# Second SwiGLU stage of a hybrid layer: the high weights meet both operand parts in one 512-column matmul

## The chip, the core and the metric

The kernel runs on one core of a Trainium2 chip. The metric is the device time of one execution in microseconds (us). TensorE (PE) multiplies; a matmul holds 128x128 weights that a separate weight load (PEld) has put there, and streams the columns of the other operand past them into a bank of PSUM. VectorE (DVE) and ScalarE (ACT) read PSUM and SBUF, each working through its own queue in order. GpSimd (POOL) has no part in the stage that is changed. SyncE (SP) issues the DMAs.

## The reference

One layer on x of 256 tokens by 1024 features, in float32: a SwiGLU stage, a mixer (a diagonal state-space branch and an attention branch), a second SwiGLU stage, a final norm.

```python
def swiglu(h, w_gate, w_up, w_down):
    return (jax.nn.silu(h @ w_gate) * (h @ w_up)) @ w_down
...
    h = rmsnorm(x, ffn1_norm[l])
    x = x + 0.5 * swiglu(h, ffn1_w_gate[l], ffn1_w_up[l], ffn1_w_down[l])
    h = rmsnorm(x, mix_norm[l])
    x = x + hybrid_mixer(h, w_in[l], ...)
    h = rmsnorm(x, ffn2_norm[l])
    x = x + 0.5 * swiglu(h, ffn2_w_gate[l], ffn2_w_up[l], ffn2_w_down[l])
return rmsnorm(x, final_norm)
```

The inner width D_FF is 2816, so each of the stage's three weight matrices is 8 x 22 = 176 tiles of 128x128.

## The kernel before

Activations lie with features on the partitions and the 256 tokens (T) along the columns. Every float32 operand of a large product is split into a high part that TensorE's fp32r format holds exactly and the low rest: weights into `wh` and `wl`, activations into `xh` and `xl` (stage input, tile `xhl`) or `ah` and `al` (gated product, tile `ahl`). A weight tile then takes three matmuls of 256 columns into the same PSUM bank, wh·xh, wh·xl and wl·xh, lines 188 to 190 of `mm3`; called a triple here. wl·xl is left out.

The weights come from HBM as one stream of units, 8 tiles (512 KB) each, in the order in which they are used. ScalarE makes `wh` of a unit (line 90, `wh<-stage`) and VectorE `wl` (line 78, `wl<-stage,wh`). `weight(n)` calls `ahead(u)` when TensorE's program reaches unit u; that issues wh of unit u+4, wl of unit u+3, the load of unit u+6 and the postponed subtractions `al = gs - ah`. Both rings hold five units. The order of the instructions on each engine is the order in which the code is written (`manual_schedule`).

The second SwiGLU stage is `ffn(f2, idle, FH2, 4, after_ffn2, 2)`, with g = 2, one part and kh = 22. A gate or an up product takes 8 weight tiles (K = 1024), which is one unit, and goes to a bank of its own: gate products to `ps_m` (`mm`, 3 banks), up products to `ps_a` (`mma`, 3 banks). The first four products (gate 0, up 0, gate 1, up 1) run interleaved over k. Then come gate 2 and up 2; two weight tiles into up 2, `catch_up` spreads the norm's factor over the partitions (`ips`, copied to `inv`) and the six products that are waiting are worked off: gate bank times inv, Silu, times up bank, copy to `ah`:

```python
            def finish(j, gs, up):
                tt(gs, gs, up)
                act(ah[:, j, :], gs)
                deferred.append(lambda o=al[:, j, :], a=gs, b=ah[:, j, :]: tt(o, a, b, ALU.subtract))

            def gated(gp):
                gs = ev.tile([128, T], F32, name="gs", tag="gs", bufs=3)
                tt(gs, gp, inv)
                act(gs, gs, AF.Silu)
                return gs
```

From gate 3 on each product is worked off when it ends. After the 22 pairs come eight down products of 22 tiles (2.75 units) each, whose results are scaled into `dn` (line 87) and added to x (tile `xg`). Products are numbered from 0 here.

Of the kernel before, what the change touches and what calls it, by code (L numbers as in the profile page):

```python
# [10 lines left out]
F32 = mybir.dt.float32  # L11
# [3 lines left out]
ALU = mybir.AluOpType  # L15
# [3 lines left out]
T = 256  # L19
D = 1024  # L20
KD = D // 128
# [12 lines left out]
X_AT = (48, 48, 48)  # L34
A_AT = (48, 0, 0)
# [26 lines left out]
def hybrid_layer(ctx: ExitStack, tc: tile.TileContext, xT, wst, consts, bc, out):  # L62
    nc = tc.nc
    V, S, G, PE = nc.vector, nc.scalar, nc.gpsimd, nc.tensor
# [7 lines left out]
    ps_m = ctx.enter_context(tc.tile_pool(name="ps_m", bufs=3, space=PSUM))  # L72
    ps_s = ctx.enter_context(tc.tile_pool(name="ps_s", bufs=2, space=PSUM))
    ps_a = ctx.enter_context(tc.tile_pool(name="ps_a", bufs=3, space=PSUM))
    ctx.enter_context(tc.manual_schedule())

    def tt(out, a, b, op=ALU.mult, eng=None):
        (eng or V).tensor_tensor(out=out, in0=a, in1=b, op=op)  # L78
# [7 lines left out]
    def stt(out, a, s, b, op0, op1):  # L86
        V.scalar_tensor_tensor(out=out, in0=a, scalar=s, in1=b, op0=op0, op1=op1)

    def act(out, a, func=AF.Copy, **kw):
        S.activation(out=out, in_=a, func=func, **kw)  # L90
# [17 lines left out]
    inv = cp.tile([128, T], F32, name="inv")  # L108
# [57 lines left out]
    def ahead(u):  # L166
        split_hi(u + LA)
        split_lo(u + LA - 1)
        load_to(u + LA + 2)
        while deferred:  # L170
            deferred.pop(0)()
        if u in hooks:
            hooks.pop(u)()

    def weight(n, cnt=1):
        u, s = divmod(n, UT)
        if u > state["at"]:
            state["at"] = u
            if u not in state["hold"]:
                ahead(u)  # L180
        h, lo = split[u]
        return h[:, s * 128:(s + cnt) * 128], lo[:, s * 128:(s + cnt) * 128]

    pos = [0]

    def mm3(ps, n, xh, xl, start, stop):
        wh, wl = weight(n)
        PE.matmul(ps, wh, xh, start=start, stop=False)  # L188
        PE.matmul(ps, wh, xl, start=False, stop=False)  # L189
        PE.matmul(ps, wl, xh, start=False, stop=stop)  # L190

    def gemm(xh, xl, nk, ps=None, side={}):
        if ps is None:
            ps = ps_m.tile([128, T], F32, name="mm", tag="mm")
        for k in range(nk):
            mm3(ps, pos[0] + k, xh[:, k, :], xl[:, k, :], k == 0, k == nk - 1)
            if k in side:
                side[k]()
        pos[0] += nk
        return ps  # L200


    xhl = cp.tile([128, 2 * KD * T + SLACK], F32R, name="xhl")

    def placed(t, n, o):
        return [t[:, o + i * n * T:o + (i + 1) * n * T].rearrange("p (k t) -> p k t", k=n) for i in range(2)]

    xv = [placed(xhl, KD, o) for o in X_AT]

    def split_x(k, g):  # L210
        xh, xl = xv[g]
# [21 lines left out]
    def norm(pool=ps_a, tag="at", diag=True, between=None):  # L233
        ps = [pool.tile([128, 1], F32, name="nps", tag=tag) for _ in range(2)]
        terms = [acc] + squares
        squares.clear()
        for n, a in enumerate(terms):
            if between and n == len(terms) - 1:
                between()
            for i in range(2):  # L240
                for o in (0, 64):
                    PE.matmul(ps[i][o:o + 64, :], a[:, i * 128 + o:i * 128 + o + 64], ones[:, 0:1],
                              start=n == 0, stop=n == len(terms) - 1)
        v, t, y = nrm[:, 0, :], nrm[:, 1, :], inv_tm
        for i in range(2):
            ts(v[:, i:i + 1], ps[i], 1.0 / D, ALU.mult, RMS_EPS, ALU.add)
        ts(y.bitcast(I32), v.bitcast(I32), -0.5, ALU.mult, RSQRT_MAGIC, ALU.add)
        gram(t, y, v)
        stt(y, t, RSQRT_B, y, ALU.subtract, ALU.mult)
        gram(t, y, v)  # L250
        ts(v, t, -0.375 * RSQRT_A ** 5, ALU.mult, 1.25 * RSQRT_A ** 3, ALU.add)
        tt(v, v, t)
        stt(y, v, 1.875 * RSQRT_A, y, ALU.subtract, ALU.mult)
        if diag:
            diags.append(ev.tile([128, 2, 128], F32, name="dg", tag="sq"))
            for i in range(2):
                ts(diags[0][:, i, :], ident, y[:, i:i + 1], ALU.mult)
# [3 lines left out]
    def spread(pool=ps_a, tag="at", copy=V.tensor_copy):  # L261
        ps = pool.tile([128, T], F32, name="ips", tag=tag)
        PE.matmul(ps, ones, diags.pop().rearrange("p a b -> p (a b)"), start=True, stop=True)
        copy(inv, ps)
        return ps


    def psum(i):
        if i % 2:
            return ps_a.tile([128, T], F32, name="mma", tag="at")  # L270
        return ps_m.tile([128, T], F32, name="mm", tag="mm")

    def ffn(pool, bg, parts, norm_at, done, g):
        kh = KF // parts
        xh, xl = xv[g]
        for f in range(parts):
            ahl = pool.tile([128, 2 * kh * T + SLACK], F32R, name="ahl", tag="ahl")
            ah, al = placed(ahl, kh, A_AT[g])
            def finish(j, gs, up):
                tt(gs, gs, up)  # L280
                act(ah[:, j, :], gs)
                deferred.append(lambda o=al[:, j, :], a=gs, b=ah[:, j, :]: tt(o, a, b, ALU.subtract))

            def gated(gp):
                gs = ev.tile([128, T], F32, name="gs", tag="gs", bufs=3)
                tt(gs, gp, inv)
                act(gs, gs, AF.Silu)
                return gs

            for j in range(kh):  # L290
                if f == 0 and j < 2:
                    if j == 0:
                        first = [psum(i) for i in range(4)]
                        for k in range(KD):
                            for i in range(4):
                                mm3(first[i], pos[0], xh[:, k, :], xl[:, k, :], k == 0, k == KD - 1)
                                pos[0] += 1
                            if k == norm_at:
                                norm(ps_s, "s5")
                                if state["at"] in state["hold"]:  # L300
                                    ahead(state["at"])
                    if j == 0:
                        continue
                    gate = gemm(xh, xl, KD, psum(0))
                else:
                    if f > 0 or j > 2:
                        gate = gemm(xh, xl, KD, psum(0))
                        gs, side = gated(gate), {}
                        if f > 0 or j < kh - 2:
                            bg()  # L310
                    else:
                        def catch_up():
                            spread(ps_s, "s5", act)
                            for i in range(2):
                                finish(i, gated(first[2 * i]), first[2 * i + 1])
                            if state["at"] in state["hold"]:
                                ahead(state["at"])

                        side = {1: catch_up}
                    up = gemm(xh, xl, KD, psum(1), side)  # L320
                    if side:
                        gs = gated(gate)
                    finish(j, gs, up)
                if f > 0 or j < kh - 2:
                    bg()
            for m in range(KD):
                ps = gemm(ah, al, kh)
                t = ev.tile([128, T], F32, name="dn", tag="sg")
                stt(t, ps, 0.5, inv, ALU.mult, ALU.mult)
                tt(x[:, m, :], t, x[:, m, :], ALU.add)  # L330
                if f == parts - 1:
                    done(m)
                bg()
# [566 lines left out]
    with tc.tile_pool(name="tab", bufs=1) as tab:  # L900
        with tc.tile_pool(name="f1", bufs=1) as f1:
            gen = s5_build(f1, tab)
            next(gen)

            def after_ffn1(m):
                split_x(m, 1)
                square(m, m == 0)


            calls = [0]  # L910

            def bg():
                calls[0] += 1
                if calls[0] > BG_FROM:
                    next(gen, None)

            ffn(f1, bg, FH1, 6, after_ffn1, 0)
            for _ in gen:
                pass
        with tc.tile_pool(name="mx", bufs=1) as mxp:  # L920
            mixer(mxp, tab)
    with tc.tile_pool(name="f2", bufs=1) as f2:
# [22 lines left out]
        for h in range(2):  # L945
            o = f2.tile([128, 2, 512], F32, name=f"out{h}")
# [115 lines left out]
```

## Time and profile before

| what | value |
|---|---|
| time, median of 3 runs | 558.54 us (558.08 to 563.71) |
| the profiled execution's own time | 557.2 us |
| its span, first to last instruction | 555.3 us |
| mean granted clock of TensorE | 0.995 |
| TensorE busy, weight loads busy | 544.5 us (98%), 534.5 us (96%) |
| VectorE busy, ScalarE busy | 399.2 us (72%), 309.1 us (56%) |
| first matmul of the second SwiGLU stage | 364.47 us |
| last start of a matmul of its down products | 545.09 us |

The span and everything in the trace are of the one profiled execution; 1.9 us of its time lie outside the span. Matmuls overlap in their pipeline, so the pace of a stream of them is read from the distance of two starts, not from the duration of one.

### The profile page before, as it was taken

The page shows a single profiled execution, that of the slowest core. Times are in us where ns is not written, and L with a number is a line of the kernel's source. Part 1 is how long each engine was busy: PE and PEld are TensorE (multiplying, and loading weights), DVE is VectorE, ACT ScalarE, POOL GpSimd, SP SyncE. Part 2 cuts the span into 40 slices and gives each one's busy share as a digit, 9 for nine tenths or more (in the row PEclk, how much of TensorE's full clock was granted, in tenths as well). Part 3 has the DMA queues.
Part 4 walks back from the last instruction along what each step waited for, and adds up shares of the span by engine and source line. Part 5 has one row for each costly group of instructions (what it writes and reads, how often), then busy time and mean ns, then how long its engine had stood idle before and what let it go on. Part 6 is the DMA issues. An engine that isn't in the chain of part 4 may idle for free.

```text
span 555.3 us, 11894 instructions
## 1 busy us (share of the span) xinstructions
PE 544.5 (98%) x4860; PEld 534.5 (96%) x4860; DVE 399.2 (72%) x657; ACT 309.1 (56%) x477; POOL 80.3 (14%) x150
## 2 busy tenths in 40 slices
PE   7999999999999999999999999999999999999994
PEld 7999999999999989989999999999999999999994
DVE  5886798888865776999845888786766666665643
ACT  7764546559575683336547665565555444455421
POOL 0288951957000000000000000000000000000000
PEclk9999999999999999999999999999999999999998
DMA  8876666557564445265342656564755555666502
GB/s 281 297 253 195 193 194 216 156 157 229 175 201 159 145 152 152 77 208 191 105 145 77 203 185 186 187 209 164 228 195 192 191 190 193 194 210 204 173 15 77
DMA packets 28678, 99.30 MB, mean 179 GB/s; under 512 B 3152, under 2 KB 3792, under 8 KB 28624
## 3 DMA queue, kind: packets, MB, share of 16 engines
q1 hardware_dynamic: 28624, 98.54, 55.0%
q8 instruction: 38, 0.62, 0.4%
q14 instruction: 16, 0.13, 0.1%
HBM read 97.48 MB, written 1.05 MB: 177 GB/s over the span
## 4 chain that ended last, share of the span: by engine, by line
PE 94%; DVE 3%; DMA 1%; issue 1%; SPq 0%; DVEq 0%; ACT 0%
PE mm L188 20%; PE mm L189 19%; PE mm L190 19%; PE mma L188 8%; PE mma L189 8%; PE mma L190 8%; PE bps L615 1%; PE sps L714 1%; DMA stage<-in_wst_dram 1%; PE yps L662 1%; PE ops L744 1%; DVE wl L78 1%; PE up L584 1%; PE up L586 1%; PE vp L586 1%; PE vp L585 1%
## 5 line engine op out<-in xcount | busy, mean ns | idle before, releaser
L78 DVE TENSOR_TENSOR wl<-stage,wh 128x1024 fp32r<-128x1024 f32 (+2 forms) x187 | 223.3, 1201 | 15.0 <-ACT wh L90 14.8
L90 ACT ACTIVATE wh<-stage 128x1024 fp32r<-128x1024 f32 (+2 forms) x187 | 191.5, 1030 | 56.3 <-PE mm L189 26.3
L188 PE MATMUL mm<-xhl,wh 128*128 128x256 f32 x544 | 152.1, 280 | 2.2 <-ACT wh L90 2.2
L190 PE MATMUL mm<-xhl,wl 128*128 128x256 f32 x544 | 150.9, 277 | 0.4 <-DVE wl L78 0.4
L189 PE MATMUL mm<-xhl,wh 128*128 128x256 f32 x544 | 150.4, 277 | 0.0
L188 PEld LDWEIGHTS mm<-xhl,wh 128*128 128x128 f32 x544 | 102.1, 188 | 3.5 <-ACT wh L90 2.4
L190 PEld LDWEIGHTS mm<-xhl,wl 128*128 128x128 f32 x544 | 102.2, 188 | 1.0 <-DVE wl L78 0.8
L189 PEld LDWEIGHTS mm<-xhl,wh 128*128 128x128 f32 x544 | 102.2, 188 | 0.1
L188 PE MATMUL mma<-xhl,wh 128*128 128x256 f32 x352 | 97.7, 278 | 0.0
L188 PE MATMUL mm<-ahl,wh 128*128 128x256 f32 x352 | 97.5, 277 | 0.0
L190 PE MATMUL mm<-ahl,wl 128*128 128x256 f32 x352 | 97.2, 276 | 0.0
L189 PE MATMUL mm<-ahl,wh 128*128 128x256 f32 x352 | 97.2, 276 | 0.0
L189 PE MATMUL mma<-xhl,wh 128*128 128x256 f32 x352 | 97.2, 276 | 0.0
L190 PE MATMUL mma<-xhl,wl 128*128 128x256 f32 x352 | 97.2, 276 | 0.0
L188 PEld LDWEIGHTS mm<-ahl,wh 128*128 128x128 f32 x352 | 66.1, 188 | 0.2 <-issue 0.2
L188 PEld LDWEIGHTS mma<-xhl,wh 128*128 128x128 f32 x352 | 66.1, 188 | 0.1
L189 PEld LDWEIGHTS mma<-xhl,wh 128*128 128x128 f32 x352 | 66.1, 188 | 0.1
L190 PEld LDWEIGHTS mm<-ahl,wl 128*128 128x128 f32 x352 | 66.1, 188 | 0.0
L189 PEld LDWEIGHTS mm<-ahl,wh 128*128 128x128 f32 x352 | 66.1, 188 | 0.0
L190 PEld LDWEIGHTS mma<-xhl,wl 128*128 128x128 f32 x352 | 66.0, 188 | 0.0
L90 ACT ACTIVATE gs<-gs 128x256 f32<-128x256 f32 x52 | 21.8, 418 | 54.1 <-DVE gs L78 53.8
L78 DVE TENSOR_TENSOR gs<-gs,mma 128x256 f32<-128x256 f32 x44 | 18.5, 419 | 38.5 <-PE mma L190 33.7
(214 smaller groups left out, 730.8 us busy)
## 6 DMA issues: line engine op xcount, KB each, us to landing
stage<-in_wst_dram SPq DMA_DIRECT2D x178, 512.0 KB, 3.7
stage<-in_wst_dram SPq DMA_DIRECT2D x7, 256.0 KB, 5.5
out_dram<-out SPq DMA_DIRECT2D x2, 512.0 KB, 3.2
xg<-in_xT_dram SPq DMA_DIRECT2D x3, 256.0 KB, 5.8
bct<-in_bc_dram SPq DMA_DIRECT2D x1, 512.0 KB, 5.5
cst<-in_consts_dram SPq DMA_DIRECT2D x1, 396.0 KB, 4.7
stage<-in_wst_dram SPq DMA_DIRECT2D x2, 128.0 KB, 2.5
xg<-in_xT_dram SPq DMA_DIRECT2D x1, 144.0 KB, 2.1
```

Source lines behind the costliest of these rows:

```text
L78: (eng or V).tensor_tensor(out=out, in0=a, in1=b, op=op)
L90: S.activation(out=out, in_=a, func=func, **kw)
L188: PE.matmul(ps, wh, xh, start=start, stop=False)
L189: PE.matmul(ps, wh, xl, start=False, stop=False)
L190: PE.matmul(ps, wl, xh, start=False, stop=stop)
L584: PE.matmul(acc2[i], xh[:, k, sl], wh, start=k == 0, stop=False)
L585: PE.matmul(acc2[i], xh[:, k, sl], wl, start=False, stop=False)
L586: PE.matmul(acc2[i], xl[:, k, sl], wh, start=False, stop=k == KD - 1)
L615: PE.matmul(bp[part][o, gp, :], Rt[part][:, 8 * h + gp, o], Uc[:, 8 * h + gp, :], start=True, stop=True)
L662: PE.matmul(ypf[64 * par:64 * par + 64, gg, :], l, r.rearrange("p a b -> p (a b)"), start=term == 0, stop=term == 2)
L714: PE.matmul(sps[e][:, blk, :].rearrange("p a b -> p (a b)"), q[r, i, qs], k[r, i, ks], start=part == 0, stop=part == 1)
L744: PE.matmul(op[:, i, e, :], pq[:, b, :], v[:, j, h, :], start=j == 0, stop=b != 1)
```

## The change

Only the second SwiGLU stage (g = 2) is changed. The high and the low part of its operands are laid side by side for each k (`paired`), so that one 512-column matmul `wh · [xh | xl]` writes wh·xh into the first half of a bank and wh·xl into the second; `wl · xh` stays a 256-column matmul into the first half (`mmw`, `gemmw`). A triple thus becomes a pair, with two weight loads in place of three. For the first k of a product the wide matmul comes first, for the others the narrow one. Each result now is the sum of a bank's halves, made by `fold`: ScalarE copies the second half to SBUF, VectorE adds the first. That is done for the 44 gate and up products and for seven of the eight down products; the last down product keeps the triples. 352 + 7 x 22 = 506 triples are replaced, and 51 folds added.

```diff
@@ mm3, after it
+    def mmw(ps, n, y, start, stop):
+        wh, wl = weight(n)
+
+        def high():
+            PE.matmul(ps, wh, y, start=start, stop=stop)
+
+        if start:
+            high()
+        PE.matmul(ps[:, 0:T], wl, y[:, 0:T], start=False, stop=False)
+        if not start:
+            high()
+
+    def gemmw(y, nk, ps, side={}):
+        for k in range(nk):
+            mmw(ps, pos[0] + k, y[:, k, :], k == 0, k == nk - 1)
+            if k in side:
+                side[k]()
+        pos[0] += nk
+        return ps
@@ placed, after it
+    def paired(t, n, o):
+        return t[:, o:o + 2 * n * T].rearrange("p (k t) -> p k t", k=n)
+
+    def halves(y):
+        return y[:, :, 0:T], y[:, :, T:]
+
+    xw = paired(xhl, KD, X_AT[2])
+    xv = [placed(xhl, KD, o) for o in X_AT[:2]] + [halves(xw)]
@@ ffn
+            def fold(ps):
+                if g < 2:
+                    return ps
+                c = pool.tile([128, T], F32, name="fold", tag="fold", bufs=4)
+                act(c, ps[:, T:])
+                tt(c, ps[:, 0:T], c, ALU.add)
+                return c
+
+            def product(i, side={}):
+                if g < 2:
+                    return gemm(xh, xl, KD, psum(i), side)
+                return gemmw(xw, KD, psum(i, 2 * T), side)
...
-                tt(gs, gs, up)
+                tt(gs, gs, fold(up))
...
-                tt(gs, gp, inv)
+                tt(gs, fold(gp), inv)
...
-                ps = gemm(ah, al, kh)
+                if g < 2 or m == KD - 1:
+                    ps = gemm(ah, al, kh)
+                else:
+                    ps = fold(gemmw(aw, kh, psum(0, 2 * T)))
```

On TensorE, at the catch-up in up 2, there stood before (names are tiles: `mma` the bank of up 2, `ips` the spread norm factor):

```order
L188 MATMUL mma<-xhl,wh 128x256
L189 MATMUL mma<-xhl,wh 128x256
L190 MATMUL mma<-xhl,wl 128x256
L263 MATMUL ips<-dg,ones 128x256
L188 MATMUL mma<-xhl,wh 128x256
```

and now stands:

```order
L196 MATMUL mma<-xhl,wh 128x512
L200 MATMUL mma<-xhl,wl 128x256 x2
L196 MATMUL mma<-xhl,wh 128x512
L290 MATMUL ips<-dg,ones 128x256
L200 MATMUL mma<-xhl,wl 128x256
```

The two narrow matmuls with `wh` have become one wide one; the place of `ips` in the stream is the same.

On VectorE, at the catch-up, the last two of the six waiting products, and what follows them, before (`gs` the gated value, `wl` the low weights of a unit, `ahl` the postponed subtractions):

```order
L78 TENSOR_TENSOR gs<-mm,inv 128x256
L78 TENSOR_TENSOR gs<-gs,mma 128x256
L78 TENSOR_TENSOR wl<-stage,wh 128x1024
L78 TENSOR_TENSOR ahl<-gs,ahl 128x256 x3
L78 TENSOR_TENSOR gs<-mm,inv 128x256
L78 TENSOR_TENSOR wl<-stage,wh 128x1024
```

and now:

```order
L78 TENSOR_TENSOR fold<-mm,fold 128x256
L78 TENSOR_TENSOR gs<-fold,inv 128x256
L78 TENSOR_TENSOR fold<-mma,fold 128x256
L78 TENSOR_TENSOR gs<-gs,fold 128x256
L78 TENSOR_TENSOR wl<-stage,wh 128x1024
L78 TENSOR_TENSOR ahl<-gs,ahl 128x256 x3
L78 TENSOR_TENSOR fold<-mm,fold 128x256
L78 TENSOR_TENSOR gs<-fold,inv 128x256
L78 TENSOR_TENSOR wl<-stage,wh 128x1024
```

An add stands ahead of each use of a product; six of them have come in ahead of the first `wl` after the catch-up.

On ScalarE, at the same place, before:

```order
L90 ACTIVATE inv<-ips 128x256
L90 ACT_TABLE_LOAD
L90 ACTIVATE gs<-gs 128x256
L90 ACTIVATE ahl<-gs 128x256
```

and now:

```order
L90 ACTIVATE inv<-ips 128x256
L90 ACTIVATE fold<-mm 128x256
L90 ACT_TABLE_LOAD
L90 ACTIVATE gs<-gs 128x256
L90 ACTIVATE fold<-mma 128x256
L90 ACTIVATE ahl<-gs 128x256
```

A copy has come in ahead of each Silu and of each copy to `ahl`. From gate 3 on ScalarE now has, for a gate product and the making of wh on either side of it:

```order
L90 ACTIVATE wh<-stage 128x1024
L90 ACTIVATE fold<-mm 128x256
L90 ACTIVATE gs<-gs 128x256
L90 ACTIVATE wh<-stage 128x1024
```

The copy stands behind the `wh` of one unit and ahead of that of the next.

## Rows read from the trace of the kernel before

**Rows 1.** The page's busy times by engine, and its chain by engine.

```profile
PE 544.5 (98%) x4860; PEld 534.5 (96%) x4860; DVE 399.2 (72%) x657; ACT 309.1 (56%) x477; POOL 80.3 (14%) x150
...
PE 94%; DVE 3%; DMA 1%; issue 1%; SPq 0%; DVEq 0%; ACT 0%
```

**Rows 2.** Busy time by window: gate and up products after the catch-up; down products.

```profile
core 0: us, PE busy (x) PEld busy (x) DVE busy (x) ACT busy (x) POOL busy (x), PEclk, DMA share, GB/s
382.01:486.00 103.99, 103.99 (x920) 103.99 (x919) 67.92 (x103) 53.87 (x81) 0.00 (x0) 1.00 0.58 189
486.00:545.20 59.20, 59.20 (x524) 59.17 (x523) 30.55 (x40) 25.28 (x33) 0.00 (x0) 1.00 0.45 141
```

**Rows 3.** The chain in order of time: start, length, what; every third matmul shown.

```profile
423.42 0.11 PE mma L189
...
431.92 0.11 PE mm L189
```

**Rows 4.** Timeline of PE, the mixer's 512-column matmuls and those behind them.

```profile
238.35 0.39 PE L584 MATMUL vp<-wh,xhl 128*128 128x512 f32 x1
238.58 0.39 PE L585 MATMUL vp<-wl,xhl 128*128 128x512 f32 x1
...
249.34 0.28 PE L188 MATMUL mm<-xhl,wh 128*128 128x256 f32 x1
...
249.93 0.28 PE L190 MATMUL mm<-xhl,wl 128*128 128x256 f32 x1
```

**Rows 5.** Timeline of PEld, a weight load beside them.

```profile
238.35 0.19 PEld L585 LDWEIGHTS vp<-wl,xhl 128*128 128x128 f32 x1
```

**Rows 6.** The chain in order of time, the norm's two matmul passes in up 2.

```profile
379.68 0.43 PE ips L263 x2
```

**Rows 7.** Timeline of ACT at the catch-up, idle time and its releaser in brackets.

```profile
380.15 0.39 ACT L90 ACTIVATE inv<-ips 128x256 f32<-128x256 f32 x1 [0.17 <-PE ips L263]
380.56 1.28 ACT L90 ACT_TABLE_LOAD   x1
381.85 0.42 ACT L90 ACTIVATE gs<-gs 128x256 f32<-128x256 f32 x1
382.76 0.42 ACT L90 ACTIVATE ahl<-gs 128x256 fp32r<-128x256 f32 x1 [0.49 <-DVE gs L78]
383.09 0.42 ACT L90 ACTIVATE gs<-gs 128x256 f32<-128x256 f32 x1
...
385.56 1.05 ACT L90 ACTIVATE wh<-stage 128x1024 fp32r<-128x1024 f32 x1
```

**Rows 8.** Timeline of DVE at the catch-up.

```profile
380.57 0.42 DVE L78 TENSOR_TENSOR gs<-mm,inv 128x256 f32<-128x256 f32 x1 [2.00 <-ACT inv L90]
382.30 0.42 DVE L78 TENSOR_TENSOR gs<-gs,mma 128x256 f32<-128x256 f32 x1 [1.30 <-ACT gs L90]
382.64 0.42 DVE L78 TENSOR_TENSOR gs<-mm,inv 128x256 f32<-128x256 f32 x1
...
385.12 1.22 DVE L78 TENSOR_TENSOR wl<-stage,wh 128x1024 fp32r<-128x1024 f32 x1
386.25 1.09 DVE L78 TENSOR_TENSOR ahl<-gs,ahl 128x256 fp32r<-128x256 f32 x3
```

**Rows 9.** Timeline of PE, the first matmul of gate 3 and of up 4.

```profile
382.00 0.28 PE L188 MATMUL mm<-xhl,wh 128*128 128x256 f32 x1
...
390.16 0.28 PE L188 MATMUL mma<-xhl,wh 128*128 128x256 f32 x1
```

**Rows 10.** Timeline of DVE in the down products, an operation and the one that reads its result.

```profile
493.04 0.42 DVE L87 SCALAR_TENSOR_TENSOR dn<-mm,inv 128x256 f32<-128x256 f32 x1 [2.50 <-PE mm L190]
493.50 0.42 DVE L78 TENSOR_TENSOR xg<-dn,xg 128x256 f32<-128x256 f32 x1
```

**Rows 11.** Timeline of ACT, two makings of wh back to back.

```profile
367.47 1.99 ACT L90 ACTIVATE wh<-stage 128x1024 fp32r<-128x1024 f32 x2
```

**Rows 12.** Waits from 371 us on: who waited for whom, us in total, times, longest.

```profile
DVE dn L87 <- PE mm L190: 22.6, 8, 6.3
...
ACT wh L90 <- PE mm L189: 13.5, 10, 1.7
```

More of the change, by code (lines that the diff above doesn't have):

```diff
@@ L206, in placed @@
         return [t[:, o + i * n * T:o + (i + 1) * n * T].rearrange("p (k t) -> p k t", k=n) for i in range(2)]
-    xv = [placed(xhl, KD, o) for o in X_AT]
+    def paired(t, n, o):
[4 more added lines that the diff above has]
+    xv = [placed(xhl, KD, o) for o in X_AT[:2]] + [halves(xw)]
     def split_x(k, g):
@@ L265, in spread, with psum @@
         return ps
-    def psum(i):
+    def psum(i, w=T):
         if i % 2:
-            return ps_a.tile([128, T], F32, name="mma", tag="at")
-        return ps_m.tile([128, T], F32, name="mm", tag="mm")
+            return ps_a.tile([128, w], F32, name="mma", tag="at")
+        return ps_m.tile([128, w], F32, name="mm", tag="mm")
     def ffn(pool, bg, parts, norm_at, done, g):
@@ L277, in ffn @@
             ahl = pool.tile([128, 2 * kh * T + SLACK], F32R, name="ahl", tag="ahl")
-            ah, al = placed(ahl, kh, A_AT[g])
+            if g == 2:
+                aw = paired(ahl, kh, A_AT[g])
+                ah, al = halves(aw)
+            else:
+                ah, al = placed(ahl, kh, A_AT[g])
+            def fold(ps):
[9 more added lines that the diff above has]
+                return gemmw(xw, KD, psum(i, 2 * T), side)
             def finish(j, gs, up):
-                tt(gs, gs, up)
+                tt(gs, gs, fold(up))
                 act(ah[:, j, :], gs)
@@ L292, in ffn @@
                     if j == 0:
-                        first = [psum(i) for i in range(4)]
+                        first = [psum(i, T if g < 2 else 2 * T) for i in range(4)]
                         for k in range(KD):
                             for i in range(4):
-                                mm3(first[i], pos[0], xh[:, k, :], xl[:, k, :], k == 0, k == KD - 1)
+                                if g < 2:
+                                    mm3(first[i], pos[0], xh[:, k, :], xl[:, k, :], k == 0, k == KD - 1)
+                                else:
+                                    mmw(first[i], pos[0], xw[:, k, :], k == 0, k == KD - 1)
                                 pos[0] += 1
@@ L303, in ffn @@
                         continue
-                    gate = gemm(xh, xl, KD, psum(0))
+                    gate = product(0)
                 else:
                     if f > 0 or j > 2:
-                        gate = gemm(xh, xl, KD, psum(0))
+                        gate = product(0)
                         gs, side = gated(gate), {}
@@ L319, in ffn @@
                         side = {1: catch_up}
-                    up = gemm(xh, xl, KD, psum(1), side)
+                    up = product(1, side)
                     if side:
@@ L326, in ffn @@
             for m in range(KD):
-                ps = gemm(ah, al, kh)
+                if g < 2 or m == KD - 1:
+                    ps = gemm(ah, al, kh)
+                else:
+                    ps = fold(gemmw(aw, kh, psum(0, 2 * T)))
                 t = ev.tile([128, T], F32, name="dn", tag="sg")
```

## The prediction

> **What bounds the kernel now.** I first read the page's busy times and its chain by engine [rows 1]: TensorE is busy 98% of the span and holds 94% of the chain that ended last. Weight loads are busy 96%, but a load lies beside a matmul, so that share alone does not say which of the two sets the pace. Next the stage that is changed, by windows [rows 2]: from gate 3 to the last down product TensorE and its loads have no gap, VectorE works 67.92 of 103.99 us (65%) and ScalarE 53.87 (52%) among the gate and up products, less among the down products, and the granted clock is 1.00, the upper of its two levels (2.4 GHz). So nothing but the pace of the matmul stream counts here, as long as VectorE and ScalarE deliver weights and free banks in time.
>
> The pace is read from starts. In the chain every third matmul of this stage starts 0.34 us after the last: from 423.42 to 431.92 are 25 triples [rows 3], 8.50 / 25 = 0.340 us for a triple, 113.3 ns for a matmul of 256 columns. It is the same in both halves of the stage. That of 512 columns can be read too, since the mixer has such matmuls with the same number format: 48 of them start between 238.35 and 249.34 [rows 4], 10.99 / 48 = 229.0 ns each. The load for the next one starts with the running one, at 238.35, and takes 0.19 us [rows 5], so it is over before the 0.229 us are: these wide matmuls do not wait for loads.
>
> **The change on TensorE.** A triple (340.0 ns) becomes a narrow and a wide matmul. By these rows 113.3 + 229.0 = 342.3 ns, 2.3 ns more, times 506 = **+1.2 us**. The columns are the same 768, and two narrow ones cost 226.7 ns against 229.0 for a wide one: what falls away is a weight load that was hidden. That is the whole of it for TensorE's own work; the eight tiles of a unit take 2.738 us in place of 2.720.
>
> Bounds of this term, since no row has a narrow and a wide matmul in turn. Above: right behind the mixer's wide matmuls the narrow ones start 118 ns apart (five from 249.34 to 249.93 [rows 4]) before they fall back to 113; if that were lasting, 229 + 118 = 347 ns, +7 x 506 = +3.5 us. Below: the shortest time in the trace for a pass of that size is the norm's, two passes in 0.43 us [rows 6], 215 ns each, in another number format; 215 + 113.3 = 328.3, -11.7 x 506 = -5.9 us. I don't let the narrow one become shorter, since a load starts only with the matmul ahead of it, and a narrow matmul leaves it 113 ns. I take the 229.0, as those rows have this format, this column count and this bank size.
>
> The Trainium skill, page "TensorE: Matmul & The Clock Gate", section "Back-to-back issue gap", gives a warm matmul its columns over the clock and a fixed 2.5 ns, 215.7 ns for 512 columns; with it the term would be about -5.6 us. The trace of this kernel does not agree for the format used here: 229.0 ns.
>
> **The change on ScalarE and VectorE: where covered.** 51 copies and 51 adds of 0.42 us come in (21 us on each engine). Down products: VectorE waits 22.6 us there for TensorE, up to 6.3 at a time [rows 12], and ScalarE waits 13.5 us for a free place in the ring of wh; seven folds of about 0.9 us vanish in that. The last down product has no fold, so the end after it is unchanged: 0. Banks: gate 3 needs the bank of gate 0. That add starts 0.42 behind the first copy, which stands 0.33 behind the copy to inv at 380.15 (steps below), at 380.90, and is over by 381.3; gate 3 starts at 382.00 [rows 9]. Margin 0.7 us, and later ones have more: 0.
>
> In the steady part the order on ScalarE is copy, Silu (or copy to `ahl`), wh, and between the first two VectorE must do the add and the multiply. I add up one round from starts. Copy from PSUM to VectorE's start: 380.15 to 380.57 = 0.42 [rows 7, 8]. An operation on VectorE to the one that reads it: 493.04 to 493.50 = 0.46 [rows 10]. VectorE to ScalarE: 382.30 to 382.76 = 0.46. ScalarE to its next: 382.76 to 383.09 = 0.33. Making wh to what is behind it: 1.99 - 1.05 = 0.94 [rows 7, 11]. Round: 0.42 + 0.46 + 0.46 + 0.33 + 0.94 = 2.61 us for a unit, against 2.74 us of TensorE. It holds, with 0.13 us to spare. VectorE's own share of a round is 0.46 + 0.34 + 1.13 (`wl`, 385.12 to 386.25 [rows 8]) and 0.34 for a postponed subtraction in every second: 2.27 at most, no bound.
>
> **Where it is not covered: the catch-up in up 2.** Six products wait for inv and are then worked off ahead of the next `wh` and `wl`. Before, that takes until `wl` starts at 385.12 and wh at 385.56 [rows 7, 8]. Now each product costs ScalarE and VectorE a full chain: next on ScalarE 0.33, copy to add 0.42, add to multiply 0.46, multiply to ScalarE 0.46, together 1.67 us. Gate 0: copy at 380.15 + 0.33 = 380.48, the table load 0.41 later (as from 380.15 to 380.56), Silu 1.29 after that: 382.18. Four chains (up 0, gate 1, up 1, gate 2) end in Silu at 388.86. Up 2: copy 389.19, add 389.61, multiply 390.07, then `wl` 0.34 later at 390.41, done 1.22 later at 391.63. The order on VectorE shows that this `wl` is the first after the catch-up; it is that of the unit three ahead of gate 3, up 4. TensorE came to up 4 at 390.16 [rows 9]. Now its stream is later by 48 triples of 2.3 ns and three units of 18 ns, 0.17, and the first wide matmul needs only wh, 0.23: it wants `wl` at 390.56. The chain is moved as well, by 0.10 with `ips`: 391.73. TensorE waits **1.17 us**.
>
> The next `wl` (gate 5) stands behind three subtractions (1.02), add (0.46) and multiply (0.34): `wl` at 390.51 + 1.13 + 1.02 + 0.80 = 393.46, done at 394.68. TensorE wants it at 390.33 + 2.74 + 1.17 + 0.23 = 394.47: another **0.21 us**. After that the rounds of 2.61 us gain on the units of 2.74, and no more waits follow. wh is needed a unit later than `wl` and starts at 390.96 for gate 5: no wait. Together +1.4 us, between 0.7 and 2.1 if each of the twelve steps on the way is 0.05 us off.
>
> **Sum.** +1.2 + 1.4 = +2.6 us. The profiled execution would go from 557.2 to 559.8. The median of the runs shown is 1.3 us above that execution; on it the sum is 558.5 + 2.6 = **561.1 us**, +0.5%.
>
> **The rivals.** *The wide matmul runs at the clock's pace*, 215 ns in place of 229: the stage's stream loses 5.9 us. For it: the norm's passes [rows 6]. Against it: 48 wide matmuls of this very format [rows 4]. The catch-up starts with `ips` in the same stream and so is moved with it; against it only six triples at 11.7 ns (0.07) and three units at 0.094 (0.28) come sooner, so the first wait is 1.6 us in place of 1.17, the second 0.3, together 1.9, and a unit then takes 2.63 us, just over the round of 2.61. Result -5.9 + 1.9 = -4.0: 554.5 us. Chance 0.10. It is also the time that the skill's rule on the issue gap would give.
>
> *ScalarE's round becomes the bound* and the kernel gets slower for good. For it: only 0.13 us to spare, and a round crosses engines twice, each in order. Against it: each step has its row. It decides from 2.74 us on. If each of the five steps takes 0.05 us more, a round is 2.86, TensorE waits 0.12 in each of the 34 units from gate 5 to the last up product, +4.1: 558.5 + 2.6 + 4.1 = 565.2 us. Chance 0.13.
>
> *The change does nothing to the stream and nothing waits*: the 1.4 us are covered, because the steps are quicker in a burst or up 4 comes later than I think. Then 558.5 + 1.2 = 559.7 us, inside the forecast's own range; chance 0.15, counted with it below.
>
> **How the numbers follow.** The forecast with this last case has 0.74; its range is from -0.3 + 0.7 (a wide matmul as two narrow ones, 226.7, is the lower end that I believe) to +3.5 + 2.1, 558.9 to 564.1 us. The two rivals have 0.10 and 0.13, what I haven't thought of 0.03. The runs before differ by 0.1% between the lower two and 1% to the highest, and about 1% is what a measurement of this kernel can tell from no change. A range that holds the time 8 times in 10 takes the forecast's, 1.5 us below and above for what separates one set of runs from another and the near parts of both rivals: 556.5 to 565.5 us. Within 1% is 552.9 to 564.1: the forecast and most of the first rival, 0.79. Slower by over 1%: the second rival and the forecast's upper end, 0.15. Faster by over 1%: the first rival without its wait, 0.06.
>
> **What the profile after would show.** In the stage, wide matmuls 0.23 us and narrow ones 0.11 us apart, 0.342 together; 0.33 would be the first rival. The first 'idle' of TensorE in the stage is at up 4, near 390.6 us, 1.2 us long, put down to VectorE's `wl`, and a short one at gate 5; waits for `wl` at every unit up to the last up product would be the second rival, and then ScalarE would have no idle time between gate 5 and the down products. `wl` behind the catch-up starts at 390.5 in place of 385.12. Weight loads fall by 506, with no gain in time. The span from the last down product to the end is unchanged. I am wrong if a wide and a narrow matmul in turn have a pace that neither has alone, which no row of before shows.

## The result, and the profile after

| | before | after |
|---|---|---|
| median | 558.31 us (556.24 to 563.71, 6 runs) | 564.69 us (564.21 to 569.94, 6 runs) |
| the profiled execution, its span | 557.2 us, 555.3 us | 564.53 us, 562.8 us |
| mean granted clock | 0.995 | 0.997 |

After over before is 1.0131 (95% interval 1.0092 to 1.0169): the kernel is slower by 1.3%, and the span has grown by 7.5 us. A few executions of either kernel lie some 5 us above the rest (562.25 and 563.71 before; 569.94 after, at a granted clock of 0.996); none of them was traced, and what they are stays open.

The page of after, busy times by engine and its chain by engine, against [rows 1]:

```profile
PE 552.3 (98%) x4354; PEld 518.4 (92%) x4354; DVE 421.3 (75%) x708; ACT 324.1 (58%) x528; POOL 80.0 (14%) x150
...
PE 92%; DVE 4%; ACT 1%; DMA 1%; issue 1%; SPq 0%; DVEq 0%
```

506 matmuls and 506 loads are gone, and the loads are busy 16.1 us less. TensorE is still busy 98% of a longer span. The windows of [rows 2], of after:

```profile
core 0: us, PE busy (x) PEld busy (x) DVE busy (x) ACT busy (x) POOL busy (x), PEclk, DMA share, GB/s
382.01:486.00 103.99, 103.39 (x588) 89.53 (x587) 82.34 (x139) 63.65 (x119) 0.00 (x0) 1.00 0.54 179
486.00:545.20 59.20, 59.20 (x339) 51.50 (x338) 36.40 (x50) 29.84 (x44) 0.00 (x0) 1.00 0.48 160
```

Loads now have gaps (89.53 of 103.99 us), VectorE and ScalarE have more work and are still far from full, and the granted clock is 1.00, the upper level (2.4 GHz), as before. TensorE idles for 0.6 us in the first window and not at all in the second. So most of the 7.5 us is no wait: the same columns go through more slowly. Starts of after in the timeline of PE, the first seven down products (154 pairs) and then the last one (triples):

```profile
490.52 0.40 PE L196 MATMUL mm<-ahl,wh 128*128 128x512 f32 x1
...
544.84 0.28 PE L188 MATMUL mm<-ahl,wh 128*128 128x256 f32 x1
...
548.73 0.28 PE L188 MATMUL mm<-ahl,wh 128*128 128x256 f32 x1
...
550.50 0.28 PE L188 MATMUL mm<-ahl,wh 128*128 128x256 f32 x1
```

154 pairs take 54.32 us, 352.7 ns a pair against 340.0 ns for a triple [rows 3]. From 548.73 to 550.50 are five triples of the last product, in code that the change leaves as it was: 1.77 / 5 = 354 ns, where a triple took 340. Inside the pairs, in up 7:

```profile
409.63 0.28 PE L200 MATMUL mma<-xhl,wl 128*128 128x256 f32 x1
409.75 0.40 PE L196 MATMUL mma<-xhl,wh 128*128 128x512 f32 x1
409.98 0.28 PE L200 MATMUL mma<-xhl,wl 128*128 128x256 f32 x1
...
411.04 0.28 PE L200 MATMUL mma<-xhl,wl 128*128 128x256 f32 x1
```

A narrow matmul takes 118 ns and a wide one 235; four pairs 1.41 us. The sum: 12.7 ns x 506 pairs = 6.4 us; the last product's 66 narrow matmuls at 118 instead of 113.3, 0.3 us; and one wait, at up 4:

```profile
391.06 0.40 PE L196 MATMUL mm<-xhl,wh 128*128 128x512 f32 x1
392.06 0.51 PE L200 MATMUL mma<-xhl,wl 128*128 128x256 f32 x2 [0.59 <-DVE wl L78]
```

1.00 us from a wide matmul to the next one, where 0.235 is usual: 0.76 us. 6.4 + 0.3 + 0.76 = 7.5 us, the growth of the span.

### The profile page after: what moved, and what is told of

The parts are those of the page before. It is cut to its first block, busy times and chain, and to the rows that moved or that the text cites. A ratio compares the mean times of both kernels' runs of the same rounds, so it can differ in the third digit from the quotient of the medians.

```text
span 562.8 us, 10955 instructions
## 1 busy us (share of the span) xinstructions
PE 552.3 (98%) x4354; PEld 518.4 (92%) x4354; DVE 421.3 (75%) x708; ACT 324.1 (58%) x528; POOL 80.0 (14%) x150
## 4 chain that ended last, share of the span: by engine, by line
PE 92%; DVE 4%; ACT 1%; DMA 1%; issue 1%; SPq 0%; DVEq 0%
PE mm L196 13%; PE mm L188 13%; PE mm L190 13%; PE mm L189 12%; PE mma L196 7%; PE mm L200 7%; PE mma L188 4%; PE mma L190 4%; PE mma L189 4%; PE mma L200 3%; PE bps L666 1%; DVE wl L78 1%; PE sps L765 1%; DMA stage<-in_wst_dram 1%; PE yps L713 1%; PE ops L795 1%
## 5 line engine op out<-in xcount | busy, mean ns | idle before, releaser
L188 PE MATMUL mm<-xhl,wh 128*128 128x256 f32 x368 | 103.8, 282 | 1.0 <-ACT wh L90 1.0
L190 PE MATMUL mm<-xhl,wl 128*128 128x256 f32 x368 | 102.4, 278 | 0.6 <-DVE wl L78 0.6
L189 PE MATMUL mm<-xhl,wh 128*128 128x256 f32 x368 | 102.1, 277 | 0.0
L188 PEld LDWEIGHTS mm<-xhl,wh 128*128 128x128 f32 x368 | 69.3, 188 | 2.5 <-ACT wh L90 1.4
L190 PEld LDWEIGHTS mm<-xhl,wl 128*128 128x128 f32 x368 | 69.4, 189 | 1.2 <-DVE wl L78 1.2
L189 PEld LDWEIGHTS mm<-xhl,wh 128*128 128x128 f32 x368 | 69.4, 189 | 0.1
L196 PE MATMUL mma<-xhl,wh 128*128 128x512 f32 x176 | 64.5, 396 | 0.0
L196 PE MATMUL mm<-xhl,wh 128*128 128x512 f32 x176 | 64.5, 396 | 0.0
L188 PE MATMUL mm<-ahl,wh 128*128 128x256 f32 x198 | 55.1, 278 | 0.0
L189 PE MATMUL mm<-ahl,wh 128*128 128x256 f32 x198 | 54.8, 277 | 0.0
L196 PE MATMUL mm<-ahl,wh 128*128 128x512 f32 x154 | 54.0, 397 | 0.0
L188 PE MATMUL mma<-xhl,wh 128*128 128x256 f32 x176 | 49.0, 279 | 0.0
L189 PE MATMUL mma<-xhl,wh 128*128 128x256 f32 x176 | 48.7, 277 | 0.0
L200 PE MATMUL mm<-xhl,wl 128*128 128x256 f32 x176 | 46.3, 282 | 0.0
L90 ACT ACTIVATE ahl<-gs 128x256 fp32r<-128x256 f32 x44 | 18.4, 418 | 37.5 <-DVE gs L78 37.1
```

The costliest lines, as they stand in the source:

```text
L196: PE.matmul(ps, wh, y, start=start, stop=stop)
L200: PE.matmul(ps[:, 0:T], wl, y[:, 0:T], start=False, stop=False)
```

## The experiments

The first theory was formed from the last product's triples: **the stream has two paces**, 113 and 118 ns for 256 columns at the same granted clock; what has run ahead chooses between them, and the alternation of wide and narrow matmuls brings the longer one. The rivals: the layout (both parts side by side) makes reads slower; the width itself does (a wide matmul is slow and drags its neighbour along); the folds' reading of the banks slows TensorE's writing. Ratios are over the kernel before, run on the same chip: e1 to e3 on one (before 557.73 us), e4 to e6 on a second (557.16), e7 on a third (556.83). A tile is the pair or the triple of one weight tile.

| kernel | median us | ratio (95%) | pace of a tile in the stage |
|---|---|---|---|
| e1_triples_paired | 557.21 | 0.9984 (0.9949 to 1.0019) | 0.340 us |
| e2_wide_split | 564.57 | 1.0134 (1.0110 to 1.0158) | 0.353 us |
| e3_no_folds | 563.54 | 1.0112 (1.0092 to 1.0132) | 0.353 us |
| e4_wides_first | 561.74 | 1.0078 (1.0048 to 1.0108) | 0.347 us |
| e5_one_wide_product | 563.27 | 1.0115 (1.0049 to 1.0181) | 0.353 us |
| e6_narrows_in_twos | 563.83 | 1.0112 (1.0053 to 1.0172) | both paces, mixed |
| e7_wide_then_turn | 557.43 | 1.0009 (0.9996 to 1.0022) | 0.340 us |

**e1_triples_paired: the new layout alone.** Triples on operands that lie side by side, no folds.

```diff
-        ...
-        PE.matmul(ps[:, 0:T], wl, y[:, 0:T], start=False, stop=False)
+        PE.matmul(ps, wh, y[:, 0:T], start=start, stop=False)
+        PE.matmul(ps, wh, y[:, T:], start=False, stop=False)
+        PE.matmul(ps, wl, y[:, 0:T], start=False, stop=stop)
```

> The changed kernel with its operands laid side by side as in the change, but with the three 256-column matmuls of before and no folds; the result is complete. Two theories for the pace of 0.353 us for a pair of matmuls in the changed stage (a triple had 0.340). Theory 'layout': the two parts lying side by side make the stream slow, whatever the width; then a triple takes 0.353 us here too and the time is about 6.8 us over the kernel before. Theory 'width': 512-column matmuls in turn with 256-column ones make it slow; then a triple takes 0.340 us and the time is that of before within 0.5 us.

Its chain in order of time, the first of every third matmul shown:

```profile
419.98 0.11 PE mma L195
...
426.44 0.11 PE mm L195
```

19 triples in 6.46 us, 0.340 each, and no difference in the time. The layout costs nothing.

**e2_wide_split: the width without the layout.** The wide matmul reads xh and xl from their old places, two pieces of 256 columns.

```diff
-        return t[:, o:o + 2 * n * T].rearrange("p (k t) -> p k t", k=n)
+        return t[:, o:o + 2 * n * T].rearrange("p (a k t) -> p k a t", a=2, k=n)
```

> The change with the operand parts where the kernel before has them, all high parts ahead of all low parts; the 512-column matmul reads two pieces of 256 columns. Theory 'layout': the pair of a narrow and a wide matmul takes about 0.340 us and the time is that of before plus the wait of some 0.8 us at up 4. Theory 'width': 0.353 us as in the changed kernel, and its time, 6 to 7 us over before.

The whole loss is there: wide matmuls 235 ns, narrow ones 118, and 0.98 us ahead of up 4. So it comes with the wide matmuls in the stream, wherever their operand lies.

**e3_no_folds.** The halves are not added, everything else as in the change.

```diff
             def fold(ps):
-                if g < 2:
-                    return ps
+                return ps[:, 0:T]
```

> The changed kernel without copies and adds: only the first half of each bank is read, so the product of high weights and low operand parts is left out of the result. Both theories on the pace keep 0.353 us a pair. The folds' own cost shows as what goes away: the trace of the changed kernel has one gap of 0.76 us ahead of up 4, so 0.8 us less than the changed kernel if that gap is all that they cost; the rival of the prediction, in which ScalarE's round sets the pace of the stage, wants several us less and shorter distances between matmuls everywhere.

The timeline of PE, at up 4:

```profile
391.40 0.40 PE L196 MATMUL mm<-xhl,wh 128*128 128x512 f32 x1
391.64 0.40 PE L196 MATMUL mma<-xhl,wh 128*128 128x512 f32 x1
```

The wait is gone (0.24 us from the last matmul of gate 4 to up 4) and the pace is that of the change, 118 and 235 ns. The span is 0.5 us under that of the change, the median 1.15 us, with intervals that overlap: the 51 folds cost at most about 1 us of the loss, and their reading of banks does not slow TensorE.

**m1_streams: the streams by themselves.** The layer is replaced by streams of 24 weight tiles in which, from the second stream on, nothing waits: triples on either layout, pairs, wide matmuls only, narrow ones only, pairs in other orders. Ahead of a stream stands a full float32 matmul, a float32 matmul of 64 weight columns with a single column to stream, or nothing.

```diff
+    stream("tfarb", rest, triples(fh, fl))
+    stream("tneara", full, triples(yh, yl))
+    stream("tnearb", rest, triples(yh, yl))
+    stream("paira", full, pairs(y, "nwnw"))
+    stream("tfarc", None, triples(fh, fl))
+    ...
+    stream("tnearc", None, triples(yh, yl))
```

> Streams of matmuls by themselves, 24 weight tiles each, with no work on the other engines; the layer's computation is left out. Theory 'layout': triples on parts side by side (tneara) take 0.353 us, triples on parts far apart (tfara) 0.340. Theory 'width': both 0.340, and the pair of narrow and wide (paira) 0.353. A third theory, 'state': the stream has two paces, 113 and 118 ns for 256 columns, and what ran ahead of it sets which; then tfara, behind a full float32 matmul, differs from tfarb, behind a 64-column one, and the triples right behind pairs (tfarc, tnearc) are slow. Streams of only wide and of only narrow matmuls (wides, narrows), without change of the moving operand (wsame, nsame), in another order (wfirst, group) and with other offsets of the operand (offo, offp, offq) show which of them alone is slow.

The views of single tiles: count, then least, median and most ns of one, first and last start. In these traces the duration tells the pace too: a narrow matmul reads 276 ns where starts lie 113 ns apart (as in e7 from 385.89 on, below) and 281 where they lie 118 apart.

```profile
L925 PE MATMUL tfarb<-far,wl x24: 276/276/278, 33.1 to 40.9; 128*128 128x256 f32 x24
...
L925 PE MATMUL tneara<-near,wl x24: 279/281/281, 41.7 to 49.8; 128*128 128x256 f32 x24
...
L925 PE MATMUL tnearb<-near,wl x24: 276/276/286, 50.6 to 58.4; 128*128 128x256 f32 x24
...
L940 PE MATMUL paira<-near,wh x24: 388/397/585, 58.8 to 67.2; 128*128 128x512 f32 x24
...
L924 PE MATMUL tfarc<-far,wh x24: 280/281/281, 67.5 to 75.7; 128*128 128x256 f32 x24
```

One and the same code has two paces: `tneara` and `tnearb` differ only in the matmul ahead of them, and the triples right behind pairs (`tfarc`, `tnearc`) keep the longer pace to their last matmul, 72 in each. Streams with no wide matmul have it too (`narrows`, 118 ns throughout). The comparison of `tfara` with `tfarb` that was planned fell out: `tfara`, the first stream, waited for its operands, and some of its matmuls lie 213 ns apart. Pairs took 352 ns, with the operand at three other places in SBUF 350, in two other orders 347 and 353. Wide matmuls alone took 233 ns, with the token columns as weights 226 to 232: about 226 at the least, which is what two narrow ones take.

**e5_one_wide_product: one product of pairs, everything else triples.** Only gate 3 is done as the change does it, 8 pairs and one fold; the other 498 are triples as before.

```diff
-                if g < 2:
+                state["product"] = state.get("product", 0) + (g == 2)
+                if g < 2 or state["product"] != 3:
                     return gemm(xh, xl, KD, psum(i), side)
```

> The kernel before on the side-by-side layout, with narrow and wide matmuls and a fold in one product alone, gate 3; the other 65 products of the stage keep three matmuls of 256 columns, and the result is complete. Theory 'alternation': a narrow matmul is slow only where wide ones stand between; eight pairs are slow, +0.1 us, and every triple behind takes 0.340 us. Theory 'state': wide and narrow matmuls in turn put the stream into the slower of two paces, and a plain stream of triples behind them keeps it; then the 472 triples from up 3 on take 0.353 us, +6.3 us, nearly what the whole change costs.

The timeline of PE behind gate 3, and then the chain in order of time 36 us later:

```profile
384.23 0.40 PE L196 MATMUL mm<-xhl,wh 128*128 128x512 f32 x1
384.46 0.28 PE L188 MATMUL mma<-xhl,wh 128*128 128x256 f32 x1
...
385.52 0.28 PE L188 MATMUL mma<-xhl,wh 128*128 128x256 f32 x1
```

```profile
419.96 0.12 PE mma L188
...
426.67 0.12 PE mma L188
```

Three triples in 1.06 us right behind it, and 19 in 6.71 us (0.353) further on: from the end of gate 3 to the last down product, 1416 matmuls from 384.46 to 551.12, the stream stays at the longer pace. Eight wide matmuls cost nearly what 506 cost. A wide matmul that drags its own neighbour along can't do that, nor can 51 folds.

**e7_wide_then_turn: the same, and a change of pace behind it.** e5, with one 128x128 float32 transpose into a spare bank behind gate 3.

```diff
+                ps = gemmw(xw, KD, psum(i, 2 * T), side)
+                PE.transpose(ps_s.tile([128, 128], F32, name="turn", tag="s5"), x[:, 0, 0:128], ident)
+                return ps
```

> The kernel of the one wide product (gate 3 in eight pairs, all else of the stage in triples) with one 128x128 float32 transpose into a spare bank right behind that product; the result is complete. Theory 'state': among the streams alone a transpose ended the slow pace that pairs had left (td), so the triples from up 3 on take 0.340 us again and the time is that of the kernel before, +0.2 us for the transpose and eight slow pairs. If instead the wide product costs by its fold, its bank or its place, the transpose changes nothing and the time stays 6 us over before.

Its timeline of PE at the transpose, and its chain later:

```profile
384.85 0.27 PE L324 MATMUL turn<-cst,xg 128*128 128x128 f32 x1
...
385.89 0.28 PE L190 MATMUL mma<-xhl,wl 128*128 128x256 f32 x1
386.00 0.28 PE L188 MATMUL mma<-xhl,wh 128*128 128x256 f32 x1
```

```profile
420.17 0.11 PE mma L188
...
426.29 0.11 PE mm L188
```

From 385.89 on starts lie 0.11 apart, 18 triples later on take 6.12 us, and 1408 matmuls in a row keep that pace to 545.35. The time is that of before, 557.43 us (ratio 1.0009), against 563.27 (1.0115) without the transpose. The wide matmuls, the fold and the layout are the same in both; only the pace of what follows differs. That settles that the loss of e5 is this pace; in the change the pairs themselves show it, 352.7 ns each.

**e4_wides_first: no alternation.** The eight wide matmuls of a unit first, then its eight narrow ones.

```diff
+            for k in ks:
+                PE.matmul(ps, weight(pos[0] + k)[0], y[:, k, :], start=k == 0, stop=False)
+            for k in ks:
+                PE.matmul(ps[:, 0:T], weight(pos[0] + k)[1], y[:, k, 0:T], start=False, stop=k == nk - 1)
```

> The changed kernel with the eight weight tiles of a unit in another order: all eight wide matmuls, then the eight narrow ones; the result is complete. Theory 'alternation': no wide and narrow one in turn any more, wides 0.2333 us as in the stream of wides alone, narrows 0.113: 0.347 for a pair, +3.4 us over before and the wait at up 4. Theory 'state': the narrow ones keep the pace that the wides leave, 0.118: 0.351, +5.6 us and the wait.

The timeline of PE, a unit's narrow matmuls, the wide ones of the next and the next narrow ones:

```profile
402.20 1.07 PE L212 MATMUL mm<-xhl,wl 128*128 128x256 f32 x8
403.12 2.02 PE L210 MATMUL mma<-xhl,wh 128*128 128x512 f32 x8
404.98 0.62 PE L212 MATMUL mma<-xhl,wl 128*128 128x256 f32 x4
```

Eight narrow ones take 0.92 us, 115 ns each, eight wide ones 1.86, 232.5 each: 347 ns a tile, half of the loss. A narrow matmul behind another is mostly back at 113 to 114, which I had not expected so soon behind wide ones: 347 ns is the number of 'alternation', and 'state' missed with 351. There is also a new wait of 0.7 us ahead of gate 3, for the fold of the bank that it takes.

**e6_narrows_in_twos.** Two narrow, two wide in turn.

```diff
+            for c in "wnnw" if k0 == 0 else "nnww":
```

> The changed kernel in the order narrow, narrow, wide, wide; the result is complete. In the changed kernel's trace the second of two narrow matmuls and the wide one behind it, once in each product, took 113 and 226 ns, the others 118 and 235. If that is what two alike in a row do, half of the pairs here take 0.339 us and half 0.353: 0.346, +3.1 us over before and the wait at up 4, 3.6 us less than the changed kernel. If it hangs on the place in the product instead, the time is that of the changed kernel.

The timeline of PE in up 4 and up to gate 5:

```profile
394.94 0.40 PE L213 MATMUL mma<-xhl,wl 128*128 128x256 f32 x2
...
395.65 0.40 PE L213 MATMUL mma<-xhl,wl 128*128 128x256 f32 x2
...
396.34 0.39 PE L213 MATMUL mma<-xhl,wl 128*128 128x256 f32 x2
```

Two tiles take 0.71 us (394.94 to 395.65) and 0.69 (395.65 to 396.34), where two pairs take 0.71: the first wide one of two mostly runs at 226 ns and the second at 231 to 236, and of the narrow ones too mostly one of two is at the shorter pace. From the first down product to the last matmul of the stage it is 60.85 us, against 61.98 in the change and 59.73 before, half of the loss, as the pattern says. In the gate and up products it is 125.06 us, against 125.98 in the change and 120.89 before: boundary matmuls of 121 ns and a wait of 0.86 us at up 4 leave only 0.9 us there. Together the stage is 2.0 us shorter than in the change, where 3.6 were expected. The four runs, 562.65 to 567.20 us, do not show that: the one that was profiled (564.82 us) lost 2.3 us ahead of the stage, which begins at 366.88 in place of 364.54. TensorE waited there for 2.15 us until 8.3, and its granted clock was 0.51 from 8 to 15 us, the lower level (1.2 GHz), where the trace of the change has 1.00.

**m2_states: what sets the pace.** Triples of 16 tiles, behind pairs with one thing between, then behind a few matmuls of other widths.

```diff
+    for name, gap in (("ta", None), ("tb", rest), ("tc", full), ("td", turn), ("te", idle(0)), ("tf", idle(3))):
+        stream("p" + name, None, p, 8)
+        stream(name, gap, fast, 16)
+    ...
+    for name, n, cols in (("th", 1, 512), ("ti", 2, 512), ("tj", 3, 512), ("tk", 1, 128), ("tl", 2, 128), ("tm", 1, 384),
+                          ("tn", 2, 384), ("to", 1, 64)):
+        stream(name, put(n, cols), fast, 16)
```

> Streams of triples by themselves, 16 weight tiles each, behind different things; the layer's computation is left out. Theory 'state': behind 8 pairs the triples take 118 ns a matmul with nothing between (ta), and some of a 64-column matmul (tb), a full float32 one (tc), a transpose (td), an idle time of 1 or 4 us (te, tf) bring back 113. Behind a fast stream, one, two or three wide matmuls or a few of other widths (th to to) show whether a single wide one is enough to slow what follows. Theory 'alternation': all of these streams take 113.

The views of single tiles:

```profile
L924 PE MATMUL tb<-far,wh x16: 281/281/281, 37.2 to 42.5; 128*128 128x256 f32 x16
...
L924 PE MATMUL td<-far,wh x16: 276/276/281, 54.4 to 59.6; 128*128 128x256 f32 x16
...
L924 PE MATMUL th<-far,wh x16: 280/281/281, 91.0 to 96.3; 128*128 128x256 f32 x16
...
L924 PE MATMUL ti<-far,wh x16: 280/281/281, 97.1 to 102.4; 128*128 128x256 f32 x16
...
L924 PE MATMUL tj<-far,wh x16: 276/276/276, 103.5 to 108.6; 128*128 128x256 f32 x16
```

Behind pairs the float32 matmul of 64 weight columns leaves the longer pace (`tb`), the transpose ends it (`td`), as do the full float32 matmul and 1.4 us of idle time. None of these sets the pace for sure: in m1_streams the 64-column one stood between `tneara` at the longer and `tnearb` at the shorter pace, and the full one ahead of `tneara` and `narrows`, both at the longer. The stream with nothing between (`ta`) tells nothing: the pairs ahead of it waited, its first matmuls lie 213 ns apart, and it ended at 113. One single wide matmul puts a stream at the shorter pace into the longer one for all its 48 matmuls (`th`); two more change nothing (`ti`), three more bring it back (`tj`).

**m3_counts: is it the number?** Each of 21 numbers and widths put between two streams of 8 tiles, with a transpose ahead of the first.

```diff
+    for i, (n, cols) in enumerate(((1, 512), (2, 512), (3, 512), (4, 512), (5, 512), (6, 512), (1, 256), (2, 256), (3, 256),
+                                   (1, 128), (2, 128), (3, 128), (4, 128), (1, 384), (2, 384), (3, 384), (1, 320), (1, 448),
+                                   (1, 192), (1, 480), (1, 496))):
+        stream("r" + c, turn, fast, 8)
+        stream("t" + c, put(n, cols), fast, 8)
```

> Streams of eight triples behind a transpose (fast), then one to six matmuls of another width, then eight triples again; the layer's computation is left out. Theory 'count': it hangs on how many matmuls of 512 columns are put in; then one and two slow what follows and three do not, and the widths between 128 and 496 show no rule of their own. Theory 'columns': it hangs on the sum of the columns put in, so 4 x 128 acts as 1 x 512, and 2 x 256 too, which are the stream's own matmuls and cannot slow it. At the end pairs with triples behind them, three times, to see whether the slow pace comes each time.

One wide matmul (`ra` before it, `ta` behind it) and three (`rc`, `tc`):

```profile
L924 PE MATMUL ra<-far,wh x8: 281/281/281, 41.8 to 44.3; 128*128 128x256 f32 x8
...
L925 PE MATMUL ta<-far,wl x8: 276/276/282, 45.0 to 47.4; 128*128 128x256 f32 x8
...
L925 PE MATMUL rc<-far,wl x8: 276/276/279, 53.9 to 56.3; 128*128 128x256 f32 x8
...
L925 PE MATMUL tc<-far,wl x8: 281/281/282, 57.3 to 59.8; 128*128 128x256 f32 x8
```

The premise fell: behind the transpose the stream is at the shorter pace in only 9 of 21 cases, so it is no sure reset, and in e7 it was one outcome in one place. Where the stream ahead of the transpose was at the longer pace, it stayed there in 10 of 11 cases (three of them at the end of the run). For wide matmuls in a row there is a pattern: an odd number exchanges the two paces, in whichever the stream was, an even number keeps it, nine of nine over m2_states and m3_counts. 256 columns keep it (three of three, all at the longer pace). Behind 384 columns it was the shorter one each time (five of five); the other widths (128 to 496) show no rule. It mostly fits e4, where the narrow ones behind eight wide ones in a row stay at the shorter pace from up 3 on. It does not explain alternation: pairs leave the longer pace in three of three cases here, and in e5, where eight wide matmuls, an even number, are mixed with narrow ones.

## Why the prediction was wrong

The sum gave +2.6 us, 561.1 us; the median is 564.69, 6.4 over that of before, and the span grew by 7.5. That 564.69 lies inside the wide range is luck: the forecast's own ends at 564.1, and the wide one was stretched for noise and for a rival that did not come.

*Loads are hidden*: right as far as it goes. 506 fewer loads, 16.1 us less busy time on PEld, and no gain in the time.

*The change on TensorE, +1.2 us*: **the step that failed**. It added 113.3 ns and 229.0 ns from rows in which narrow matmuls follow narrow ones and wide ones wide ones, and the pair took 352.7 on average: +6.4 us, and +0.3 in the last product, which I had left unchanged. The upper bound, 347 ns "if that were lasting", was too low as well: it put the longer pace on the narrow matmul and left the wide one at 229, which is between its own two paces (226 and 235). The five narrow matmuls 118 ns apart in [rows 4] I took for a transient; they have the spacing of the second pace, which lasted for five matmuls there and for hundreds elsewhere. The trace of before has it elsewhere, in code that is plain triples: a down product of the first stage, timeline of PE of before,

```profile
171.52 0.28 PE L189 MATMUL mm<-ahl,wh 128*128 128x256 f32 x1
...
175.17 0.28 PE L190 MATMUL mm<-ahl,wl 128*128 128x256 f32 x1
```

32 starts, 3.65 us / 31 = 117.7 ns, at the granted clock of the rest. Had I read the pace of triples in all stages and not in this stage alone, I would have seen that it is not a property of the instruction, and the upper bound would have been 117.7 + 2 x 117.7 = 353 ns, +6.6 us. That plain triples can run at the longer pace stood in the trace; that alternation brings it could only be tried. The range's lower end has a slip besides: -0.3 us for a wide matmul of 226.7 ns, where 226.7 + 113.3 = 340.0 is no change at all.

*The Trainium skill*, page "TensorE: Matmul & The Clock Gate", section "Back-to-back issue gap", gives as the gap of an isolated matmul its columns over the clock and 2.5 ns, about 216 ns for 512 columns. No stream here reaches that; wide matmuls take about 226 to 236 ns.

*The wait at up 4, 1.17 us*: right mechanism, right place, 0.76 us. `wl` was late by the chain as worked out, and the rest is in the timelines of DVE and ACT of after:

```profile
390.78 1.22 DVE L78 TENSOR_TENSOR wl<-stage,wh 128x1024 fp32r<-128x1024 f32 x1
```

```profile
382.69 0.42 ACT L90 ACTIVATE gs<-gs 128x256 f32<-128x256 f32 x1
...
385.97 0.42 ACT L90 ACTIVATE gs<-gs 128x256 f32<-128x256 f32 x1 [0.95 <-DVE gs L78]
...
395.17 0.36 ACT L90 ACTIVATE fold<-mma 128x256 f32<-128x256 f32 x1
...
397.75 0.36 ACT L90 ACTIVATE fold<-mm 128x256 f32<-128x256 f32 x1
```

Two chains of the catch-up take 3.28 us, 1.64 each (forecast 1.67), and `wl` starts at 390.78 (forecast 390.5). It is done at 392.00, 0.27 later than I said, but the slower stream wants it at 391.06 + 0.235 = 391.29, 0.73 later: 1.17 + 0.27 - 0.73 = 0.71. The 0.21 us at gate 5 became 0.01 for the same reason.

*Folds elsewhere are covered*: right, no other wait appears, and e3 puts all folds at about 1 us at most. *ScalarE's round*: 2.58 us (forecast 2.61) against units that take 2.83 and not 2.74. That rival was not what made it slower. *The rival of 215 ns* fell with 235; the passes of [rows 6] that spoke for it have 256 columns each, in another format, and were no price for 512. The sentence "I am wrong if a wide and a narrow matmul in turn have a pace that neither has alone" names the place, but each has that pace alone too; what the change does is to put the stream into it and keep it there.

Open: what in the chip the two paces are, and why alternation leads to the longer one. 0.340 and 0.3533 us are 816 and 848 cycles of 2.4 GHz for 768 columns; the runs show no cause. Both kernels have as many weight loads as matmuls (4860 before, 4354 after) and no stream does without them, so whether the loads have a part in it is untested. Triples show one sign: at the longer pace one of three loads takes 192 ns and the others 187 or 188, at the shorter pace all take 187 or 188 (e5 and before from 400 to 420 us); pairs at the longer pace do not show it. Nor did any order of wide and narrow matmuls come below 340 ns a tile.

## What to carry to other kernels

Before adding up durations from a trace, read the pace of the same instruction in several stages: two values at one granted clock mean that it is no property of the instruction alone, and the longer one belongs in the range. A stream that bounds the kernel can be slowed for its whole length by a few instructions of another shape ahead of it, so look at the code behind an edit that was not edited. Fewer and wider matmuls gained nothing here, where weight loads lay beside matmuls and the cost went by columns.

## What the hardware showed that was not expected

Eight alternating pairs slow some 1,400 matmuls behind them by 4%, at a granted clock of 1.00: +6.1 us over before in e5, +0.6 in e7, each on its own chip. One matmul of 512 columns can do the same to 48 that follow (`th`), and one ahead of a stream at the longer pace took it back (`ta` of m3_counts). A 128x128 float32 transpose ended it in e7_wide_then_turn and in m2_states (`td`), but in only one of 11 cases in m3_counts, and in 5 of 13 there a stream at the shorter pace ran at the longer one behind it.
